# A two-layer decoder trunk: VectorE's steps of a pair in the up projection put in another order, one low part given to GpSimd, and the first two tiles of the down projection split earlier

## The chip, the core and the metric

One Trainium2 chip, one of its cores. The metric is the device time of one execution of the whole program in microseconds (us), the median of several runs. Engines: PE is TensorE (matmuls, with its weight loads), ACT is ScalarE, DVE is VectorE, POOL is GpSimd, and SP is SyncE, which issues the DMAs here. PE writes PSUM only; its eight banks are the tiles `pg` (four) and `pa` (four), each 128 x 512 in f32.

## The reference, cut to what matters

```python
def conv_ffn(h, w_up, conv_w, conv_b, w_down):
    u = causal_dwconv(h @ w_up, conv_w, conv_b)          # width 3
    a, g = jnp.split(u, 2, axis=-1)
    return (jax.nn.gelu(g, approximate=True) * a) @ w_down

for l in range(DEPTH):                                   # 2 layers
    h = hybrid_mixer(rmsnorm(x, pre_mix_g[l]), ...)
    x = x + rmsnorm(h, post_mix_g[l])
    h = memory_cross_attention(rmsnorm(x, pre_mem_g[l]), ...)
    x = x + rmsnorm(h, post_mem_g[l])
    h = conv_ffn(rmsnorm(x, pre_ffn_g[l]), w_up[l], fconv_w[l], fconv_b[l], w_down[l])
    x = x + rmsnorm(h, post_ffn_g[l])
```

512 tokens, width 1024, FFN width 2816, all in f32. The change concerns `conv_ffn` alone: `h @ w_up` (1024 to 5632 columns), the convolution over tokens with the gating, and the start of `@ w_down`.

## The kernel before, in words

**Precision.** A matmul operand is split in two fp32r parts: `hi` is a rounded copy made by ACT, `lo` is the source minus `hi`, made by DVE. `mm3` then issues three matmuls, hi.hi, hi.lo and lo.hi. A weight unit is a 128 x 1024 tile, loaded by SP into one of two `raw` buffers and split into one of five `whi` and five `wlo` buffers (`w_split`, `split`, L89 to L100).

**Up projection.** The 5632 columns are 22 pairs `j` of 128 linear columns (`a`, the unit `raws[j]`) and 128 gate columns (`g`, the unit `rgs[j]`, two buffers). Pairs 0 and 1 are done plainly (`feat_halves`). From pair 2 on, `up_products` takes a pair as a 2 x 2 block product (halves of the 1024 inputs by the two columns; tokens 0 to 255, "left", by 256 to 511, "right"), done with seven block products instead of eight. Its weight sides are `raws[j]` itself (kind `a`, products 1 and 2), the four sums of `add_up` (L1095 to L1098, on POOL: tiles `T`, kinds `t` for products 5 and 6 and `u` for 7 and 4), and half of `rgs[j]` (kind `b`, product 3, a single buffer `b`). `high(j, kind)` (L1105) casts the high part on ACT; `low(j, kind)` (L1116) subtracts on DVE. One product is 12 matmuls of 128 x 256. In iteration `j` of the loop (L1157) PE does product 5 of pair j, 4 of pair j-1, 6 of j, 1 of j+1, 2, 3 and 7 of j.

**What follows a pair.** Two PSUM tiles collect it, `A` (linear) and `G` (gate): `total(j)` alternates between two pairs of `pg` banks, so A and G of pair j are the banks of pair j-2. ACT's copy (L1161) and DVE's add (L1162) finish the right half of A and G of pair j-1; DVE's second add (L1183) prepares the left half of G of pair j, which product 3 then goes on with. `conv_first` (ACT, L1022) writes the first convolution term into `u`, `conv_rest` (DVE, L1027) adds two more from PSUM, ACT takes the gelu into G, and `gated` (DVE, L1041) multiplies into a tile of `gtiles`.

**Down projection.** `down` (L1202) takes the 22 `gtiles` in order. For tile k it splits the tile and a weight unit, then issues 24 matmuls of 128 x 512 into all eight banks: the four `pa` first, then the four `pg`, which are the banks of `total`: the first two those of pair 20, the last two those of pair 21.

**Order of work.** In `up_products` the order of ACT, DVE and POOL is the order of the code (`manual_schedule`, L1060), and so is SP's (L1062); every engine works its list in order and waits at the head. PE's order is that of the code throughout. Elsewhere a scheduler sets the order, so that pieces of the steps ahead of the loop mix with the end of `feat_halves`.

Of the kernel before, what the change touches and what calls it, by code (L numbers as in the profile page):

```python
# [23 lines left out]
NF = 22  # L24
# [14 lines left out]
def trunk_kernel(ctx: ExitStack, tc: tile.TileContext, x4, memt, w, gw, gains, mcw, fcw, gb,  # L39
# [111 lines left out]
    def run(gen):  # L151
        for _ in gen:
            tick()
# [856 lines left out]
    def ffn(l, xn, pend, forms):  # L1010
# [51 lines left out]
        with tc.manual_schedule(engines={mybir.EngineType.SP}):  # L1062
            run(up_products(l, fp, xn, forms, us, conv_first, conv_rest, gated))
        return es, order, gtiles

    def up_products(l, fp, xn, forms, us, conv_first, conv_rest, gated):
# [15 lines left out]
        def load_a(j):  # L1082
            if j < NF:
                raws[j] = load_raw(l, U_UP + 2 * j)

# [30 lines left out]
        def low(j, kind):  # L1116
            if j < NF:
                DVE.tensor_sub(ws[j, kind][1], source(j, kind), ws[j, kind][0].bitcast(F32))  # L1118
# [28 lines left out]
        for kind in "atu":  # L1147
            high(j0, kind)
            if kind != "u":
                low(j0, kind)  # L1150
# [3 lines left out]
        add_up(j0 + 1)  # L1154
        high(j0 + 1, "a")
        low(j0 + 1, "a")
        for j in range(j0, NF + 1):  # L1157
# [6 lines left out]
            load_g(j + 2)  # L1164
            load_a(j + 3)
# [7 lines left out]
            if p >= j0:  # L1173
                conv_rest(p, 1, G)
                yield from product(A[:, right], p, 4)
            low(j, "u")
            if p >= j0:
# [3 lines left out]
            if real:  # L1181
                yield from product(e1s[j], j, 6)
                DVE.tensor_add(total(j)[1][:, left], e1s[j], p5s[j])  # L1183
            high(j + 1, "t")
            low(j + 1, "t")
            if p >= j0:
                gated(p, us.pop((p, 0)), G)
            if j + 1 < NF:
# [5 lines left out]
            add_up(j + 2)  # L1194
            if real:
                yield from product(total(j)[0][:, left], j, 2)
                high(j + 1, "u")
                yield from product(total(j)[1][:, left], j, 3)
                high(j + 1, "b")
                yield from product(e1s[j], j, 7)  # L1200

    def down(l, forms, gtiles, consume, order):  # L1202
# [8 lines left out]
        for k in range(NF):  # L1211
            if k < 2:
                both = forms.flat(F32R)
                gh_, gl_ = both[:, :512], both[:, 512:]
# [4 lines left out]
            split(gtiles[k], gh_, gl_)  # L1219
            wu = load_unit(l, U_DOWN + k)  # L1220
# [18 lines left out]
    for l in range(L):  # L1239
# [30 lines left out]
        es, order, gtiles = ffn(l, xn, pend, forms)  # L1270
# [3 lines left out]
        run(down(l, forms, gtiles, tail.consume, order))  # L1274
# [83 lines left out]
```

## Time and profile before

| | us |
|---|---|
| median of 3 runs | 1593.67 |
| lowest, highest | 1593.04, 1596.27 |
| the profiled execution, its own time | 1599.54 |
| its span, first to last instruction | 1597.8 |

Busy in the span: PE 98% (a busy PE is not a PE at its peak, since matmuls are pipelined), DVE 71%, ACT 56%, POOL 22%. The up projections of the two layers run from about 480 to 685 us and from 1265 to 1464, the down projections from there to about 800 and 1577. Times in the rows further down are microseconds from the start of the span. Within a stretch the rows of one engine stand one behind the other; "[2.99 <-DVE u L1027]" is idle time of the engine just before the instruction and what ended it. In names, `wlo<-T,whi` is an instruction that writes a tile `wlo` and reads `T` and `whi`.

### The profile page before, as it was taken

To read this page: it belongs to the slowest core of one execution; us is meant where nothing else is said; L and a number is where in the kernel's file an instruction comes from. 1 tells how busy PE (TensorE), PEld (TensorE's weight loads), DVE (VectorE), ACT (ScalarE), POOL (GpSimd) and SP (SyncE) were. 2 spreads that over 40 slices of the span, in tenths; PEclk is the share of its full clock that TensorE was granted. 3 is DMA by queue.
4 is the path that set the end of the run, shared out by engine and by line. 5 is a ranking of instruction groups with operands and counts; after the bars stand their busy time and mean duration, and the time that the engine had idled before them with its cause. 6 is when DMAs were issued, how large, how long until landed. Compare 5 with 4: busy or idle time off the path is not lost.

```text
span 1597.8 us, 24498 instructions
## 1 busy us (share of the span) xinstructions
PE 1559.1 (98%) x9480; PEld 1377.3 (86%) x9480; DVE 1128.3 (71%) x1848; ACT 899.3 (56%) x1578; POOL 348.8 (22%) x252
## 2 busy tenths in 40 slices
PE   7999999999999999989999999999999999998998
PEld 5788888988899999978887888889888899997886
DVE  5687655746699999953376885557557999997433
ACT  5677574544466666642257775745445666665321
POOL 0000210100035676500010002101001567771000
PEclk9999999999999999999999999999999999999999
DMA  5422344552243332233323223444412223332321
GB/s 174 127 94 73 92 140 147 167 180 66 67 148 106 100 106 97 95 108 103 106 92 111 90 73 105 135 145 154 161 41 69 93 100 101 105 107 75 123 97 62
DMA packets 55431, 173.13 MB, mean 108 GB/s; under 512 B 6802, under 2 KB 9618, under 8 KB 55315
## 3 DMA queue, kind: packets, MB, share of 16 engines
q1 hardware_dynamic: 55314, 171.57, 33.0%
q8 instruction: 74, 1.21, 0.3%
q14 instruction: 43, 0.34, 0.1%
HBM read 165.22 MB, written 6.33 MB: 107 GB/s over the span
## 4 chain that ended last, share of the span: by engine, by line
PE 75%; DVE 11%; DMA 6%; ACT 4%; issue 2%; POOL 1%; SPq 0%; POOLq 0%; DVEq 0%; ACTq 0%
PE pg L107 47%; PE pa L107 26%; DMA raw<-in_w_dram 3%; DVE u L1027 2%; PE pa L111 2%; DVE wlo L1118 2%; DVE wlo L100 1%; ACT whi L99 1%; DMA raw<-in_memt_dram 1%; ACT junk L231 1%; DVE xg L252 1%; POOL sm L226 1%; DVE b L1118 1%; DMA raw<-dv 1%; DVE x L365 1%
## 5 line engine op out<-in xcount | busy, mean ns | idle before, releaser
L107 PE MATMUL pg<-B,whi 128*128 128x256 f32 (+1 forms) x1800 | 420.7, 327 | 8.9 <-DVE ql L991 4.0
L100 DVE TENSOR_TENSOR wlo<-raw,whi 128x1024 fp32r<-128x1024 f32 x188 | 231.3, 1231 | 223.6 <-ACT whi L99 223.2
L99 ACT CAST whi<-raw 128x1024 fp32r<-128x1024 f32 x188 | 197.6, 1052 | 226.0 <-PE pg L107 141.7
L107 PEld LDWEIGHTS pg<-B,whi 128*128 128x128 f32 x1800 | 291.0, 189 | 28.6 <-DVE ql L991 4.4
L107 PE MATMUL pg<-whi,B 128*128 128x512 f32 x896 | 297.8, 399 | 0.0
L107 PE MATMUL pg<-B,wlo 128*128 128x256 f32 (+1 forms) x896 | 288.7, 322 | 0.0
L107 PEld LDWEIGHTS pg<-whi,B 128*128 128x128 f32 x896 | 168.6, 188 | 35.1 <-DVE B L100 1.3
L226 POOL TENSOR_TENSOR sm<-sm,mhalf 128x1 f32<-128x1 f32 x56 | 34.4, 614 | 750.7 <-DVE sm L351 572.6
L107 PEld LDWEIGHTS pg<-B,wlo 128*128 128x128 f32 x896 | 168.8, 188 | 13.7
L107 PE MATMUL pg<-wlo,B 128*128 128x512 f32 x448 | 175.3, 391 | 0.6 <-DVE sm L244 0.6
L107 PE MATMUL pa<-S,whi 128*128 128x256 f32 x960 | 175.6, 283 | 0.0
L107 PEld LDWEIGHTS pa<-S,whi 128*128 128x128 f32 x960 | 148.4, 189 | 0.0
L1027 DVE SCALAR_TENSOR_TENSOR u<-pg,fcw,u 128x511 f32<-128x511 f32 (+1 forms) x176 | 130.7, 745 | 7.3 <-ACT u L1022 4.2
L107 PE MATMUL pa<-S,wlo 128*128 128x256 f32 x480 | 135.8, 283 | 0.0
L1118 DVE TENSOR_TENSOR wlo<-T,whi 128x1024 fp32r<-128x1024 f32 x80 | 125.6, 1569 | 0.0
L107 PE MATMUL pa<-whi,S 128*128 128x512 f32 x320 | 105.9, 390 | 0.0
L107 PE MATMUL pg<-whi,S 128*128 128x512 f32 x320 | 105.4, 390 | 0.0
L1022 ACT ACTIVATE u<-pg,fcw 128x512 f32<-128x512 f32 x88 | 68.6, 780 | 57.6 <-DVE pg L1162 32.0
L107 PEld LDWEIGHTS pg<-wlo,B 128*128 128x128 f32 x448 | 84.7, 189 | 15.7 <-DVE wlo L100 1.0
L107 PEld LDWEIGHTS pa<-S,wlo 128*128 128x128 f32 x480 | 90.9, 189 | 0.0
L1114 ACT CAST whi<-T 128x1024 fp32r<-128x1024 f32 x80 | 83.5, 1044 | 9.4 <-POOL T L1098 5.2
L1095 POOL TENSOR_TENSOR T<-rg,raw 128x512 f32<-128x512 f32 x40 | 55.4, 1385 | 136.7 <-DMA rg<-in_w_dram 101.6
(264 smaller groups left out, 3043.2 us busy)
## 6 DMA issues: line engine op xcount, KB each, us to landing
raw<-in_w_dram SPq DMA_DIRECT2D x228, 512.0 KB, 3.6
rg<-in_w_dram SPq DMA_DIRECT2D x40, 512.0 KB, 3.5
gain<-in_gains_dram SPq DMA_DIRECT2D x11, 512.0 KB, 5.3
raw<-in_memt_dram SPq DMA_DIRECT2D x20, 256.0 KB, 2.9
tb<-tb_d SPq DMA_DIRECT2D x16, 256.0 KB, 3.5
x<-in_x_dram SPq DMA_DIRECT2D x8, 256.0 KB, 5.7
e<-nmu_d SPq DMA_DIRECT2D x8, 256.0 KB, 3.9
dv<-vf SPq DMA_DIRECT2D x8, 256.0 KB, 4.4
```

Of the source, the lines that this page charges most:

```text
L99: ACT.copy(hi, src)
L100: DVE.tensor_sub(lo, src, hi.bitcast(F32))
L107: PE.matmul(o, lhs, rhs, **kw)
L111: PE.transpose(o, src, idn)
L226: POOL.tensor_tensor(r, v, mhalf[:, :1], ALU.pow)
L231: ACT.activation(junk[:, :src.shape[-1]], src, AF.Square, accum_out=s_)
L252: DVE.scalar_tensor_tensor(xg, xt[:, c], r, g[h], ALU.mult, ALU.mult)
L1022: ACT.activation(u, acc, AF.Identity, bias=fcw_t[:, m, 3:4], scale=fcw_t[:, m, 2:3])
L1027: DVE.scalar_tensor_tensor(u[:, q:], acc[:, :512 - q], fcw_t[:, m, 2 - q:3 - q], u[:, q:], ALU.mult, ALU.add)
L1095: POOL.tensor_tensor(t12[:, :512], b12, b11, ALU.subtract)
L1114: ACT.copy(ws[j, kind][0], source(j, kind))
L1118: DVE.tensor_sub(ws[j, kind][1], source(j, kind), ws[j, kind][0].bitcast(F32))
```

## The change

It edits `up_products` and `down` (with `ffn` and `run` only handing a list through):

- `low(j, "b")` is done by POOL instead of DVE. The other low parts stay on DVE.
- DVE's order within an iteration: the low part of `u` moves from between the two convolutions of an iteration to the end of the iteration before, behind those of `t` and `a`; the gating product of pair j-1 moves one iteration on, between the two convolutions.
- `add_up` of pair j+1 stands at the start of iteration j, behind POOL's low part of `b`; it stood in the middle of iteration j-1. SP's loads of iteration j still come after that low part and, for `raw`, after those sums.
- The weight units of down tiles 0 and 1 are loaded by the loop of the up projection, and `down_tile` splits both tiles and units in iteration 21, ahead of the last two iterations' convolution and gating.

```diff
...
@@ -1082,6 +1086,8 @@
         def load_a(j):
             if j < NF:
                 raws[j] = load_raw(l, U_UP + 2 * j)
+            elif j < NF + 2:
+                raws[j] = load_raw(l, U_DOWN + j - NF)
 
         def load_g(j):
             if j < NF:
@@ -1114,8 +1120,15 @@
             ACT.copy(ws[j, kind][0], source(j, kind))
 
         def low(j, kind):
-            if j < NF:
-                DVE.tensor_sub(ws[j, kind][1], source(j, kind), ws[j, kind][0].bitcast(F32))
+            if j >= NF:
+                return
+            sub = POOL.tensor_tensor if kind == "b" else DVE.tensor_tensor
+            sub(ws[j, kind][1], source(j, kind), ws[j, kind][0].bitcast(F32), ALU.subtract)
+
+        def down_tile(k):
+            both = forms.flat(F32R)
+            split(gtiles[k], both[:, :512], both[:, 512:])
+            return both[:, :512], both[:, 512:], w_split(raws.pop(NF + k))
 
         def total(j):
             i = 2 * (j % 2)
@@ -1146,14 +1159,13 @@
         load_a(j0 + 2)
         for kind in "atu":
             high(j0, kind)
-            if kind != "u":
-                low(j0, kind)
+            low(j0, kind)
         high(j0, "b")
         yield from first(j0)
         ACT.copy(total(j0)[0][:, left], e1s[j0])
-        add_up(j0 + 1)
         high(j0 + 1, "a")
         low(j0 + 1, "a")
+        ready = []
         for j in range(j0, NF + 1):
             p, real = j - 1, j < NF
             if p >= j0:
@@ -1162,6 +1174,7 @@
                 DVE.tensor_add(G[:, right], e1s[p], p5s[p])
             low(j, "b")
             load_g(j + 2)
+            add_up(j + 1)
             load_a(j + 3)
             if p >= j0:
                 conv_first(p, 1, G)
@@ -1172,34 +1185,37 @@
                 ACT.copy(p5s[j], e5)
             if p >= j0:
                 conv_rest(p, 1, G)
+                if p > j0:
+                    gated(p - 1, us.pop((p - 1, 0)), total(p - 1)[1])
                 yield from product(A[:, right], p, 4)
-            low(j, "u")
-            if p >= j0:
                 conv_first(p, 0, A)
                 ACT.activation(G, us.pop((p, 1)), AF.Gelu_apprx_tanh)
                 conv_rest(p, 0, A)
-            if real:
-                yield from product(e1s[j], j, 6)
-                DVE.tensor_add(total(j)[1][:, left], e1s[j], p5s[j])
+            if not real:
+                gated(p, us.pop((p, 0)), G)
+                return ready
+            yield from product(e1s[j], j, 6)
+            DVE.tensor_add(total(j)[1][:, left], e1s[j], p5s[j])
             high(j + 1, "t")
             low(j + 1, "t")
-            if p >= j0:
-                gated(p, us.pop((p, 0)), G)
-            if j + 1 < NF:
+            if j + 1 == NF:
+                ready.append(down_tile(0))
+            else:
                 yield from first(j + 1)
             high(j + 2, "a")
             low(j + 2, "a")
             if j + 1 < NF:
                 ACT.copy(total(j + 1)[0][:, left], e1s[j + 1])
-            add_up(j + 2)
-            if real:
-                yield from product(total(j)[0][:, left], j, 2)
-                high(j + 1, "u")
-                yield from product(total(j)[1][:, left], j, 3)
-                high(j + 1, "b")
-                yield from product(e1s[j], j, 7)
-
-    def down(l, forms, gtiles, consume, order):
+            yield from product(total(j)[0][:, left], j, 2)
+            high(j + 1, "u")
+            low(j + 1, "u")
+            if j + 1 == NF:
+                ready.append(down_tile(1))
+            yield from product(total(j)[1][:, left], j, 3)
+            high(j + 1, "b")
+            yield from product(e1s[j], j, 7)
+
+    def down(l, forms, gtiles, consume, order, ready):
         accs = [[pg() for _ in range(4)], [pa() for _ in range(4)]]
         held = []
 
@@ -1210,14 +1226,13 @@
 
         for k in range(NF):
             if k < 2:
-                both = forms.flat(F32R)
-                gh_, gl_ = both[:, :512], both[:, 512:]
+                gh_, gl_, wu = ready[k]
             else:
                 if k % 2 == 0:
                     both = forms.wide(F32R).rearrange("p (a b) t -> p a (b t)", a=4)
                 gh_, gl_ = both[:, k % 2, :], both[:, 2 + k % 2, :]
-            split(gtiles[k], gh_, gl_)
-            wu = load_unit(l, U_DOWN + k)
+                split(gtiles[k], gh_, gl_)
+                wu = load_unit(l, U_DOWN + k)
             if k < NF - HELD:
                 for h in (1, 0):
                     for t in range(4):
...
```

How the order of the instructions moves, at three places (line numbers of the changed kernel are 4 to 15 higher).

**DVE, one iteration of layer 0 in the middle of the loop**, from the add that finishes G to the last step before the next such add. `pg` are A and G, `u` the convolved columns, `wlo<-T` the low parts of `t` and `u`, `wlo<-raw` that of `a`, `b` that of `b`, and `B<-u,pg` the gating product. Before:

```order
L1162 TENSOR_TENSOR pg_4939<-pa_5289,p_1103_5376 128x256
L1118 TENSOR_TENSOR b_5468<-rg_5230,b_5468 128x512
L1027 SCALAR_TENSOR_TENSOR u_5489<-pg_4939,fcw_4652,u_5489 128x511
L1027 SCALAR_TENSOR_TENSOR u_5489<-pg_4939,fcw_4652,u_5489 128x510
L1118 TENSOR_TENSOR wlo_5454<-T_5308,whi_5453 128x1024
L1027 SCALAR_TENSOR_TENSOR u_5521<-pg_4938,fcw_4652,u_5521 128x511
L1027 SCALAR_TENSOR_TENSOR u_5521<-pg_4938,fcw_4652,u_5521 128x510
L1183 TENSOR_TENSOR pg_4937<-pa_5417,p_1120_5504 128x256
L1118 TENSOR_TENSOR wlo_5540<-T_5435,whi_5539 128x1024
L1041 TENSOR_TENSOR B_5415<-u_5521,pg_4939 128x512
L1118 TENSOR_TENSOR wlo_5558<-raw_5359,whi_5557 128x1024
```

And now:

```order
L1174 TENSOR_TENSOR pg_4939<-pa_5288,p_1103_5376 128x256
L1031 SCALAR_TENSOR_TENSOR u_5488<-pg_4939,fcw_4652,u_5488 128x511
L1031 SCALAR_TENSOR_TENSOR u_5488<-pg_4939,fcw_4652,u_5488 128x510
L1045 TENSOR_TENSOR B_5507<-u_5393,pg_4937 128x512
L1031 SCALAR_TENSOR_TENSOR u_5521<-pg_4938,fcw_4652,u_5521 128x511
L1031 SCALAR_TENSOR_TENSOR u_5521<-pg_4938,fcw_4652,u_5521 128x510
L1198 TENSOR_TENSOR pg_4937<-pa_5415,p_1119_5503 128x256
L1126 TENSOR_TENSOR wlo_5540<-T_5480,whi_5539 128x1024
L1126 TENSOR_TENSOR wlo_5557<-raw_5359,whi_5556 128x1024
L1126 TENSOR_TENSOR wlo_5574<-T_5481,whi_5573 128x1024
```

The low part of `b` is gone (POOL's list has it ahead of the four sums); the five steps with PSUM between the two adds stand together, and the three low parts stand behind the second add.

**DVE, layer 0, end of the loop**, from the second add of pair 21. `T<-B` and `wlo<-raw` at L100 are the low parts of the first two down tiles and their weight units. Before:

```order
L1183 TENSOR_TENSOR pg_4939<-pa_7321,p_1356_7394 128x256
L1041 TENSOR_TENSOR gt_7429<-u_7411,pg_4937 128x512
L1162 TENSOR_TENSOR pg_4939<-pa_7321,p_1356_7394 128x256
L1027 SCALAR_TENSOR_TENSOR u_7469<-pg_4939,fcw_4652,u_7469 128x511
L1027 SCALAR_TENSOR_TENSOR u_7469<-pg_4939,fcw_4652,u_7469 128x510
L1027 SCALAR_TENSOR_TENSOR u_7485<-pg_4938,fcw_4652,u_7485 128x511
L1027 SCALAR_TENSOR_TENSOR u_7485<-pg_4938,fcw_4652,u_7485 128x510
L1041 TENSOR_TENSOR gt_7490<-u_7485,pg_4939 128x512
L100 TENSOR_TENSOR T_7509<-B_4872,T_7509 128x512
L100 TENSOR_TENSOR wlo_7515<-raw_7512,whi_7514 128x1024
L100 TENSOR_TENSOR T_7542<-B_4872,T_7542 128x512
L100 TENSOR_TENSOR wlo_7548<-raw_7545,whi_7547 128x1024
```

And now:

```order
L1198 TENSOR_TENSOR pg_4939<-pa_7323,p_1357_7397 128x256
L100 TENSOR_TENSOR T_7433<-B_4872,T_7433 128x512
L100 TENSOR_TENSOR wlo_7437<-raw_7141,whi_7436 128x1024
L100 TENSOR_TENSOR T_7452<-B_4872,T_7452 128x512
L100 TENSOR_TENSOR wlo_7456<-raw_7266,whi_7455 128x1024
L1174 TENSOR_TENSOR pg_4939<-pa_7323,p_1357_7397 128x256
L1031 SCALAR_TENSOR_TENSOR u_7485<-pg_4939,fcw_4652,u_7485 128x511
L1031 SCALAR_TENSOR_TENSOR u_7485<-pg_4939,fcw_4652,u_7485 128x510
L1045 TENSOR_TENSOR gt_7489<-u_7415,pg_4937 128x512
L1031 SCALAR_TENSOR_TENSOR u_7503<-pg_4938,fcw_4652,u_7503 128x511
L1031 SCALAR_TENSOR_TENSOR u_7503<-pg_4938,fcw_4652,u_7503 128x510
L1045 TENSOR_TENSOR gt_7508<-u_7503,pg_4939 128x512
```

The four splitting steps stood behind the last gating product and now stand ahead of the add that finishes pair 21; the gating of pair 20 moved behind that add.

**DVE, layer 1, where pair 2 begins**: the last convolution terms of pairs 0 and 1 (`u<-pg`), with the low parts of pair 2 between them. Before:

```order
L1027 SCALAR_TENSOR_TENSOR u_12723<-pg_12518,fcw_12491,u_12723 128x511
L1118 TENSOR_TENSOR wlo_12817<-T_12804,whi_12816 128x1024
L1027 SCALAR_TENSOR_TENSOR u_12723<-pg_12518,fcw_12491,u_12723 128x510
L1027 SCALAR_TENSOR_TENSOR u_12754<-pg_12519,fcw_12491,u_12754 128x511
L1027 SCALAR_TENSOR_TENSOR u_12754<-pg_12519,fcw_12491,u_12754 128x510
L1041 TENSOR_TENSOR B_12728<-u_12695,u_12723 128x512
L1027 SCALAR_TENSOR_TENSOR u_12782<-pg_12520,fcw_12491,u_12782 128x511
L1027 SCALAR_TENSOR_TENSOR u_12782<-pg_12520,fcw_12491,u_12782 128x510
```

And now:

```order
L1031 SCALAR_TENSOR_TENSOR u_12723<-pg_12518,fcw_12491,u_12723 128x511
L1126 TENSOR_TENSOR wlo_12817<-T_12804,whi_12816 128x1024
L1031 SCALAR_TENSOR_TENSOR u_12723<-pg_12518,fcw_12491,u_12723 128x510
L1031 SCALAR_TENSOR_TENSOR u_12754<-pg_12519,fcw_12491,u_12754 128x511
L1126 TENSOR_TENSOR wlo_12821<-T_12805,whi_12820 128x1024
L1031 SCALAR_TENSOR_TENSOR u_12754<-pg_12519,fcw_12491,u_12754 128x510
L1045 TENSOR_TENSOR B_12728<-u_12695,u_12723 128x512
L1031 SCALAR_TENSOR_TENSOR u_12782<-pg_12520,fcw_12491,u_12782 128x511
L1031 SCALAR_TENSOR_TENSOR u_12782<-pg_12520,fcw_12491,u_12782 128x510
```

A second low part, that of `u`, stands between the last terms, three rows behind that of `t`.

## Rows read from the trace of the kernel before

**Rows 1.** Waits, PE, whole program: line waited for: us in total, times, longest.
```profile
PE pa L107 <- ACT whi L99: 6.7, 2, 3.3
PE pg L107 <- DVE pg L1183: 3.8, 8, 0.6
PE pg L107 <- DVE u L1027: 3.4, 3, 3.0
PE pa L107 <- DVE wlo L100: 2.1, 2, 1.1
```

**Rows 2.** Busy time by stage: us, PE (x) PEld DVE ACT POOL, granted clock, DMA.
```profile
692.00:694.00 2.00, 2.00 (x6) 1.55 (x5) 1.14 (x2) 0.00 (x0) 0.00 (x0) 0.50 0.81 279
...
1260.00:1270.00 10.00, 10.00 (x74) 9.92 (x74) 8.97 (x10) 7.01 (x11) 1.84 (x2) 0.87 0.32 102
...
1280.00:1455.00 175.00, 174.59 (x1455) 173.78 (x1454) 170.64 (x192) 114.69 (x173) 122.72 (x66) 1.00 0.31 103
```

**Rows 3.** Timeline, PE, end of up and start of down: start, us, instruction.
```profile
685.44 0.28 PE L107 MATMUL pg<-B,wlo 128*128 128x256 f32 x1
...
695.71 0.55 PE L107 MATMUL pg<-whi,T 128*128 128x512 f32 x1
...
1464.37 0.28 PE L107 MATMUL pg<-B,wlo 128*128 128x256 f32 x1
...
1474.48 0.39 PE L107 MATMUL pg<-whi,T 128*128 128x512 f32 x1
```

**Rows 4.** Chain of waits: start, us, PE matmuls in a row.
```profile
632.83 2.85 PE pa L107 x24
...
701.50 2.72 PE pg L107 x12
```

**Rows 5.** Timeline, ACT, copy L1161: first and last interval of each layer.
```profile
489.13 0.36 ACT L1161 COPY pg<-pa 128x256 f32<-128x256 f32 x1 [0.81 <-PE pa L107]
...
674.30 0.36 ACT L1161 COPY pg<-pa 128x256 f32<-128x256 f32 x1 [0.80 <-PE pa L107]
...
1270.84 0.36 ACT L1161 COPY pg<-pa 128x256 f32<-128x256 f32 x1 [0.81 <-PE pa L107]
...
1453.22 0.36 ACT L1161 COPY pg<-pa 128x256 f32<-128x256 f32 x1 [0.81 <-PE pa L107]
```

**Rows 6.** Groups by line: busy us, mean ns of one | idle before.
```profile
L1027 DVE SCALAR_TENSOR_TENSOR u<-pg,fcw,u 128x511 f32<-128x511 f32 (+1 forms) x176 | 130.7, 745 | 7.3 <-ACT u L1022 4.2
...
L1041 DVE TENSOR_TENSOR B<-u,pg 128x512 f32<-128x512 f32 x28 | 18.9, 676 | 0.0
...
L1183 DVE TENSOR_TENSOR pg<-pa,p 128x256 f32<-128x256 f32 x40 | 17.0, 424 | 0.0
...
L1022 ACT ACTIVATE u<-pg,fcw 128x512 f32<-128x512 f32 x88 | 68.6, 780 | 57.6 <-DVE pg L1162 32.0 <-PE pg L107 25.6
```

**Rows 7.** Timeline, DVE and POOL, layer 0: start, us, instruction.
```profile
477.14 1.31 POOL L1097 TENSOR_TENSOR T<-rg 128x512 f32<-128x512 f32 x1
...
507.32 2.08 DVE L1118 TENSOR_TENSOR wlo<-T,whi 128x1024 fp32r<-128x1024 f32 x1
508.40 2.17 POOL L1096 TENSOR_TENSOR T<-rg,T 128x512 f32<-128x512 f32 x1
...
661.03 1.22 DVE L1118 TENSOR_TENSOR wlo<-T,whi 128x1024 fp32r<-128x1024 f32 x1
...
665.05 0.68 DVE L1118 TENSOR_TENSOR b<-rg,b 128x512 fp32r<-128x512 f32 x1
```

**Rows 8.** Timeline, where the pairs begin in layers 0 and 1.
```profile
476.33 2.98 DVE L1027 SCALAR_TENSOR_TENSOR u<-pg,fcw,u 128x511 f32<-128x511 f32 x4 [1.50 <-ACT u L1022]
...
478.01 0.48 PE L107 MATMUL pg<-B,whi 128*128 128x512 f32 x1 [0.28 <-DVE u L1027]
...
1255.36 2.22 DVE L1118 TENSOR_TENSOR wlo<-T,whi 128x1024 fp32r<-128x1024 f32 x1
...
1258.38 0.47 PE L107 MATMUL pg<-B,whi 128*128 128x512 f32 x1 [2.99 <-DVE u L1027]
```

More of the change, by code (lines that the diff above doesn't have):

```diff
@@ L151, in run @@
     def run(gen):
-        for _ in gen:
+        while True:
+            try:
+                next(gen)
+            except StopIteration as end:
+                return end.value
             tick()
@@ L1062, in ffn, with up_products @@
         with tc.manual_schedule(engines={mybir.EngineType.SP}):
-            run(up_products(l, fp, xn, forms, us, conv_first, conv_rest, gated))
-        return es, order, gtiles
-    def up_products(l, fp, xn, forms, us, conv_first, conv_rest, gated):
+            ready = run(up_products(l, fp, xn, forms, us, conv_first, conv_rest, gated, gtiles))
+        return es, order, gtiles, ready
+    def up_products(l, fp, xn, forms, us, conv_first, conv_rest, gated, gtiles):
         j0 = 2
@@ L1269, in trunk_kernel @@
         forms = tail.forms
-        es, order, gtiles = ffn(l, xn, pend, forms)
+        es, order, gtiles, ready = ffn(l, xn, pend, forms)
         last = l == L - 1
@@ L1273, in trunk_kernel @@
         tail.open()
-        run(down(l, forms, gtiles, tail.consume, order))
+        run(down(l, forms, gtiles, tail.consume, order, ready))
         xn = tail.xn
```

## Prediction, made before the changed kernel ran

> **What bounds the kernel now.** I read the waits of TensorE (PE) first, then the table by stage, then single stretches of the timeline. In the table, the long middle of layer 1's up projection has PE busy in 174.59 of 175 us and VectorE (DVE) in 170.64, with GpSimd (POOL) at 122.72 [rows 2]. So PE is the bound there, DVE stands close behind it, and a change can only win what PE still loses. PE's waits list three places in the FFN [rows 1]: on ScalarE's (ACT's) `whi` and DVE's `wlo` casts, twice each (once per layer, where the down projection begins), on DVE's add L1183 eight times (inside the pairs), and on the convolution L1027 three times (where the pairs begin). After the first of these the granted clock reads 0.50, the lower level of 1.2 GHz, where the rest of the stage has the full 2.4 GHz; in 10 us after the wait at 1258 it reads 0.87 [rows 2]. Before each fall PE had stood idle, so an idle stretch is paid for twice.
>
> **The change, part by part.** PE's own order is the same in both kernels; only what the other engines do for it moves. The sum is made against the profiled execution, 1599.54 us (span 1597.8). That is 5.9 us above the median of 1593.67; I carry the difference in time over to the median; if some of the stalls below are the profiled execution's own, the gain is smaller, which the range's upper part takes in.
>
> *1. The start of the down projection.* A 128x256 matmul follows its predecessor after 2.85/24 = 0.119 us, a 128x512 one after 2.72/12 = 0.227 [rows 4]. In layer 0 the last up matmul starts at 685.44; twelve down matmuls into the `pa` banks should follow and the first into a `pg` bank start at 685.44+0.12+2.72 = 688.28. It starts at 695.71: 7.43 us lost. In layer 1: 1464.37+0.12+2.72 = 1467.21 against 1474.48, 7.27 lost [rows 3]. Together 14.7, part idle, part half clock.
> With the change both first tiles are split while PE does the last pair's products 2, 3 and 7. I count from the start of product 5 of that pair, a product taking 12 x 0.119 = 1.43. Six products end at 8.55; the copy L1161 and product 4 bring PE to about 10.6 (estimate). DVE has its add done at 6.0, four splitting subtractions, 2 x (0.68+1.22) = 3.8 [rows 7], end at 9.8. Then the add (0.42), ACT's first convolution term (0.78), two DVE terms (1.49), the gating product (0.68), two more terms and a second gating product [rows 6]: 10.2, 11.0, 12.5, 13.2, 14.7, 15.4. PE writes `pa` until 13.3, then four `pg` banks at 13.3, 14.0, 14.7 and 15.4; the last three are freed at 13.2, 14.7 and 15.4. It just fits: I leave 0.35 us per layer and book **-14.0**. Bounds: -14.7, and -12.7 if DVE comes 1 us late in each layer. The transfers come earlier too: SP issues both tiles' loads with the pairs' own and the second tile's split no longer waits behind the last gating.
>
> *2. Inside the pairs.* The copy L1161 stands once per pair. Eighteen intervals take 674.30-489.13 = 185.17 us in layer 0 and 1453.22-1270.84 = 182.38 in layer 1 [rows 5]; 84 matmuls of 0.11875 make 9.975, eighteen pairs 179.55. PE loses 5.62 and 2.83, 8.45 in all, 0.23 a pair.
> Why it loses this: product 3 starts 5 x 1.425 = 7.1 us into a pair and needs the add L1183. On DVE there stand before it an add, a low part of `b`, two convolution terms, the low part of `u`, two terms. A low part takes 1.22 alone and 2.08 when a POOL operation holds it up, and POOL's take 2.17 against 1.31 [rows 7]. Next to the convolution, which reads PSUM, POOL keeps its 1.31 [rows 7, 8]: four terms from 476.33 on take 2.98 with POOL's 1.31 at 477.14. So only the low parts collide.
> With the change the stretch is add 0.42, wait for ACT 0.78, terms 1.49, gating 0.68, terms 1.49, add 0.42 [rows 6]: 5.3, from about 0.7 to 6.0, 1.1 us ahead of product 3. The three low parts follow, 3 x 1.22, to 9.7. POOL's five operations, 5 x 1.31 = 6.5, start when the `b` cast allows, some 0.4 before the pair's first product, and end near 6.1: beside DVE's PSUM work. The sums are due when ACT casts `t` (about 4.5) and `u` (about 6.9); they are there at 3.5 and 6.1. The loads keep more than 3 us of slack: the gate's weights are asked for once POOL's low part is done and used a whole pair later. I book **-7.7** of the 8.45; bounds -8.45 and -4.
> The `b` low part costs DVE 0.68 alone [rows 7] and POOL about 1.31, as the sums show. That is 0.6 more for each of 40. The Trainium skill (GPSIMD Engine Reference, Engine selection) advises against just this: two-input elementwise work runs about twice as long on GpSimd as on VectorE. Put on the path it would be +25 us, and the sum +3; I book 0 for it, because POOL stands idle 52 of 175 us [rows 2] and product 3 needs the part only at 7.1, six microseconds after it should be done.
>
> *3. The last product 3 of each layer* comes one product sooner, at 5.7, against an add at 6.0: the longest wait of 0.6 [rows 1] shrinks to some 0.4. **-0.3**, bounds -1.0 and 0.
>
> *4. Where the pairs begin.* DVE now does the low part of `u` ahead of the last FFN convolution terms, and POOL's sums for pair 3 move behind its low part. Layer 0: DVE waited 1.50 for ACT at 476.33 [rows 8]; the low part fits in but for 0.5, so the bank PE waits for at 478.01 comes 0.5 later, and later ones up to 1.2: +0.8. Layer 1: the low part of `t` at 1255.36 took 2.22, 1.00 more than alone, because POOL was in its sums; without these PE's 2.99 us wait ends about 1 us sooner [rows 8], and perhaps the clock holds. The inserted low part then delays the fourth bank: -0.5. Together **+0.3**; bounds -1.9 (a clock that holds gives 1.5 more) and +2.2.
>
> Sum: -14.0 -7.7 -0.3 +0.3 = **-21.7**, 1593.67-21.7 = **1572.0 us**. All good bounds give -26.0, all bad ones -14.5: 1567.6 to 1579.2.
>
> **The rivals.**
> *A. The port stays full.* POOL's five operations and DVE's three low parts exclude each other for their whole length: 5 x 1.31 + 3 x 1.22 = 10.2 us, more than 9.975, and no better than today's (185.17+182.38)/36 = 10.21. Term 2 is then about -0.4, the sum -14.4: **1579.3**. For it: every collision in rows 7 costs nearly a whole operation. Against it: 10.2 counts start and end of each operation as locked, and a collision at 508 cost both engines 0.86, not 1.2 or 1.3. The Trainium skill (SBUF — State Buffer, Who interferes with whom) says that a VectorE instruction with two SBUF inputs and a GpSimd one that reads SBUF exclude each other for the whole instruction; by that rule rival A is the outcome, and the trace agrees on who collides.
> *B. Down starts, but waits one bank on.* If a tile's load or ACT is late, DVE reaches the last two gatings 2 us late or more, PE stands before the third `pg` bank, the clock falls again: half of term 1 is gone, **1579.0**. The row for it is DVE's thin fit above; against it stands that ACT's casts of both tiles are ordered ahead of all that PE waits for there.
> *C. Slower.* POOL's work spills into DVE's low parts. No POOL operation of this trace writes fp32r, so the price of the moved part is unknown. DVE's own round is 5.3+3.66 = 8.96 us; each collision adds 2.08-1.22 = 0.86. One gives 9.82, still under 9.975; from the second on DVE is the bound: two 10.68, three 11.54. Three, with term 1 kept, give 36 x (11.54-10.21) - 14 = +34, about **1628**; two give +3, **1597**. It decides when POOL ends later than about 8 us into the pair, that is when the moved part takes more than 3 us. Against it: DVE writes 512 columns of fp32r in 0.68 and of f32 in 0.676 [rows 6, 7], and POOL's work starts anew with each `b` cast, beside PSUM work.
>
> **How the numbers follow.** Forecast 0.72, A 0.11, B 0.08, C 0.06, and 0.03 that gains and losses cancel. About 0.2% (3.2 us) is what a measurement of this kernel can tell from no change. Forecast, A and B are all faster by more: 0.91. C slower, 0.06; same 0.03. The range reaches from just below the forecast's good end to past A and B: 1567 to 1581; the forecast's tails, C and the cancelling case lie outside.
>
> **What would show it.** In the changed profile: PE's waits on `whi` and `wlo` at the start of down gone and the clock 1.00 there; L1161's counterpart every 9.97 to 10.0 us; PE's waits on the second add gone except at each layer's last pair; DVE's low parts near 1.22 and POOL's operations near 1.31; POOL's low part of `b` at about 1.3. Wrong would be: low parts still at 1.6 to 2.1 in the mean (A), a wait of PE on a gating or convolution after the first twelve down matmuls (B), the moved part at 3 us or more, or pairs above 10.2 (C).

## The result, and the profile after

| | before | changed |
|---|---|---|
| median of 6 runs, us | 1594.97 (1593.04 to 1600.01) | 1575.37 (1571.36 to 1576.06) |
| profiled execution, us (span) | 1599.54 (1597.8) | 1576.06 (1574.3) |

The ratio is 0.9868, 95% interval 0.9849 to 0.9887: 19.6 us less by the medians, 21.7 forecast. The two profiled executions differ by 23.5; the one of before lay 4.6 us above its median, the changed one 0.7.

PE's waits in the changed kernel, the FFN's lines (line waited for: us in total, times, longest):

```profile
PE pg L107 <- DVE u L1031: 2.8, 2, 2.0
PE pa L107 <- DVE wlo L1126: 2.2, 2, 1.2
PE pg L107 <- ACT pg L1173: 0.9, 2, 0.4
```

The waits on `whi` and `wlo` at the start of down and those on the second add [rows 1] are gone. The wait on the convolution is still there, and one on a low part, L1126, is new: once in each layer, where the pairs begin.

Busy time by stage of the changed kernel (columns as in [rows 2]):

```profile
682.00:684.00 2.00, 2.00 (x10) 1.67 (x9) 1.97 (x4) 1.79 (x3) 0.00 (x0) 1.00 0.13 51
1240.00:1250.00 10.00, 7.87 (x50) 7.37 (x49) 9.62 (x11) 6.44 (x9) 8.25 (x6) 0.83 0.32 105
1260.00:1435.00 175.00, 175.00 (x1477) 175.00 (x1476) 138.40 (x177) 114.55 (x176) 112.18 (x88) 1.00 0.32 107
```

In 175 us of layer 1's pairs PE is never idle, and DVE is busy for 138.40 where it was for 170.64 [rows 2]. Of those 32 us the moved step would account for 17.5 x 0.68 = 12, had it run undisturbed [rows 7]; the other 20 were collisions with POOL, which have gone. The granted clock is 1.00 at the start of down, where it was 0.50. At the start of layer 1's pairs it still falls, to 0.83 in the mean.

Timeline of the changed kernel, PE at the start of down (both layers), ACT's copy (the first and the last interval of each layer, as in [rows 5]):

```profile
680.74 0.29 PE L107 MATMUL pg<-B,wlo 128*128 128x256 f32 x1
...
683.61 0.39 PE L107 MATMUL pg<-whi,T 128*128 128x512 f32 x1
...
1448.19 0.28 PE L107 MATMUL pg<-B,wlo 128*128 128x256 f32 x1
...
1451.05 0.39 PE L107 MATMUL pg<-whi,T 128*128 128x512 f32 x1
...
490.71 0.36 ACT L1173 COPY pg<-pa 128x256 f32<-128x256 f32 x1 [0.81 <-PE pa L107]
...
670.14 0.36 ACT L1173 COPY pg<-pa 128x256 f32<-128x256 f32 x1 [0.80 <-PE pa L107]
...
1258.17 0.36 ACT L1173 COPY pg<-pa 128x256 f32<-128x256 f32 x1 [0.80 <-PE pa L107]
...
1437.59 0.36 ACT L1173 COPY pg<-pa 128x256 f32<-128x256 f32 x1 [0.81 <-PE pa L107]
```

Eighteen intervals take 179.43 and 179.42 us, 9.97 a pair. From the last up matmul to the first one into a `pg` bank it is 2.87 and 2.86 us; 2.84 is what the matmuls between them take (0.12 + 12 x 0.227, [rows 4]).

Groups by line of the changed kernel (busy us, mean ns | idle before):

```profile
L1126 DVE TENSOR_TENSOR wlo<-T,whi 128x1024 fp32r<-128x1024 f32 x80 | 103.9, 1299 | 9.7 <-ACT whi L1120 9.7
L1103 POOL TENSOR_TENSOR T<-rg 128x512 f32<-128x512 f32 x40 | 54.7, 1367 | 6.4 <-DVE S L100 6.4
L1126 POOL TENSOR_TENSOR b<-rg,b 128x512 fp32r<-128x512 f32 x40 | 51.6, 1290 | 142.7 <-ACT b L1120 142.7
```

The same two groups of the kernel before:

```profile
L1118 DVE TENSOR_TENSOR wlo<-T,whi 128x1024 fp32r<-128x1024 f32 x80 | 125.6, 1569 | 0.0
...
L1097 POOL TENSOR_TENSOR T<-rg 128x512 f32<-128x512 f32 x40 | 81.0, 2025 | 11.1 <-DVE S L100 6.4 <-DVE wlo L1118 4.6
```

Low parts of `t` and `u` take 1.30 in the mean where they took 1.57, and POOL's third sum 1.37 where it took 2.03: close to the 1.22 and 1.31 of such steps undisturbed [rows 7]. The moved step takes 1.29 on POOL.

Where the two spans part, by the copies that begin the pairs: up to the first of layer 0 +1.58; its 18 intervals -5.74; the interval behind them -0.54 (9.32 became 8.78); from there to the first of layer 1 -7.97; its 18 intervals -2.96; the next -0.55; from the last copy to the end -7.32. The sum is -23.50.

### The profile page after: what moved, and what is told of

Read it like the earlier page. It is cut to its first block, busy times and chain, and to the rows that moved or that the text cites. A ratio compares the mean times of both kernels' runs of the same rounds, so it can differ in the third digit from the quotient of the medians.

```text
span 1574.3 us, 24497 instructions
## 1 busy us (share of the span) xinstructions
PE 1547.4 (98%) x9480; PEld 1371.0 (87%) x9480; DVE 1049.2 (67%) x1808; ACT 892.0 (57%) x1578; POOL 326.5 (21%) x292
## 3 DMA queue, kind: packets, MB, share of 16 engines
q8 instruction: 74, 1.21, 0.3%
## 4 chain that ended last, share of the span: by engine, by line
PE 82%; DVE 6%; DMA 5%; ACT 3%; issue 2%; POOL 1%; SPq 0%; POOLq 0%; DVEq 0%; ACTq 0%
PE pg L107 51%; PE pa L107 28%; PE pa L111 2%; DMA raw<-in_w_dram 2%; DVE wlo L100 1%; DMA raw<-in_memt_dram 1%; ACT whi L99 1%; DVE xg L256 1%; POOL sm L230 1%; ACT junk L235 1%; DVE x L369 1%; DMA raw<-dk 1%; DVE wlo L1126 1%; DMA raw<-dv 1%; DMA dk<-kf 0%
## 5 line engine op out<-in xcount | busy, mean ns | idle before, releaser
L100 DVE TENSOR_TENSOR wlo<-raw,whi 128x1024 fp32r<-128x1024 f32 x188 | 230.6, 1228 | 215.7 <-ACT whi L99 213.1
L107 PEld LDWEIGHTS pg<-B,wlo 128*128 128x128 f32 x896 | 168.9, 188 | 13.6
L1126 DVE TENSOR_TENSOR wlo<-T,whi 128x1024 fp32r<-128x1024 f32 x80 | 103.9, 1299 | 9.7 <-ACT whi L1120 9.7
L1126 POOL TENSOR_TENSOR b<-rg,b 128x512 fp32r<-128x512 f32 x40 | 51.6, 1290 | 142.7 <-ACT b L1120 142.7
```

The lines of the kernel that those rows point to most:

```text
L100: DVE.tensor_sub(lo, src, hi.bitcast(F32))
L107: PE.matmul(o, lhs, rhs, **kw)
```

## The experiments

Each kernel ran beside the kernel before, whose median was 1596.6 to 1597.6 us in these runs. I compare ratios to it; 0.001 is 1.6 us. "A pair" is the mean of the 36 intervals in the trace: 10.21 us in the kernel before, 9.97 in the changed one.

### The two halves apart

**e1_down_late**: the changed kernel without the early down tiles.

```diff
...
             high(j + 1, "t")
             low(j + 1, "t")
-            if j + 1 == NF:
-                ready.append(down_tile(0))
-            else:
+            if j + 1 < NF:
...
-            if j + 1 == NF:
-                ready.append(down_tile(1))
...
```

> The changed kernel, with the first two down tiles loaded and split where they were before, behind the last gating product; the rest of the change stays. Theory (the start of the down projection is the larger half of the gain): 14 to 15 us slower than the changed kernel, so about 1590; in the profile PE waits at the start of each down projection on ACT's and DVE's casts for 3.3 and 1.1 us, the granted clock there falls to 0.5, and the pairs stay at 9.97 us. Rival (the pairs carry the gain, the start of down is covered by them): at most 5 us slower than the changed kernel, about 1580.

Measured: 1593.5 us, ratio 0.9973 (0.9961 to 0.9985), so 0.0105 or 16.7 us above the changed kernel, where 14 to 15 was expected. Its timeline, PE at the start of down:

```profile
685.89 0.49 PE L107 MATMUL pa<-whi,T 128*128 128x512 f32 x1 [3.34 <-ACT whi L99]
...
688.28 0.80 PE L107 MATMUL pa<-wlo,T 128*128 128x512 f32 x1 [1.90 <-DVE wlo L100]
```

And the busy time by stage there:

```profile
690.00:692.00 2.00, 2.00 (x6) 1.52 (x6) 0.56 (x1) 0.23 (x1) 0.00 (x0) 0.50 0.80 242
```

Waits and half clock are back, and a pair stays at 9.97: the pairs don't depend on the early tiles. The second wait is 1.90 us where it was 1.1 at most [rows 1], so without the early tiles the new order makes the start of down a little worse than it was.

**e2_down_early_only**: the kernel before with `down_tile`, the early loads for it and the two calls of it that e1 took out.

> The kernel before, with only the early splitting of the first two down tiles added. Theory: 14 us faster than before, about 1580.5, no half clock at the start of down, and the pairs stay at 10.1 to 10.3 us in the mean. Rival (without the new order DVE is too late with the last pair, so PE waits one bank further on): 7 us faster or less, with a wait of PE on a gating product or a convolution after the first twelve down matmuls.

Measured: 1584.25 us, ratio 0.9915 (0.9898 to 0.9932): 13.6 us faster. A pair is 10.24 there, as before. The early tiles alone give 13.6 us and the pairs alone, e1's 0.0027, give 4.3: 17.9 against the 21 of 0.9868, with 2 to 3 us of uncertainty in each; e1's longer wait at the start of down takes from the 4.3.

### What the pairs owe to which part

**e3_b_on_dve**: the changed kernel with `b`'s low part on DVE.

```diff
-            sub = POOL.tensor_tensor if kind == "b" else DVE.tensor_tensor
+            sub = DVE.tensor_tensor
```

> The changed kernel, with the low part of b done by DVE again; the new order, POOL's later sums and the early down tiles stay. Order theory (what counts is that DVE's SBUF steps and POOL's steps do not meet, and DVE has room): the part fits DVE's 0.8 us wait for ACT at the start of the pair, though POOL's sums now meet it and it takes 1.2 to 1.5; pairs at 9.97 to 10.0, within 2 us of the changed kernel. Work theory (what counts is that DVE has less to do): pairs at 10.1 to 10.2, 5 to 8 us slower than the changed kernel.

Measured: 1625.12 us, ratio 1.0168 (1.0138 to 1.0198). Both theories missed: 0.68 us a pair moved back costs 1.46 a pair, which is now 11.43. One pair of it in the timeline of SP's queue, POOL, DVE and ACT:

```profile
563.25 0.33 SPq L1095 DMA_DIRECT2D rg<-in_w_dram  x1
...
567.37 1.94 POOL L1101 TENSOR_TENSOR T<-rg,raw 128x512 f32<-128x512 f32 x1 [3.03 <-DMA rg<-in_w_dram]
569.38 2.16 POOL L1102 TENSOR_TENSOR T<-rg,T 128x512 f32<-128x512 f32 x1
...
568.05 2.33 DVE L1126 TENSOR_TENSOR wlo<-raw,whi 128x1024 fp32r<-128x1024 f32 x1
570.31 2.32 DVE L1126 TENSOR_TENSOR wlo<-T,whi 128x1024 fp32r<-128x1024 f32 x1
...
570.54 0.36 ACT L1173 COPY pg<-pa 128x256 f32<-128x256 f32 x1 [0.80 <-PE pa L107]
```

The stage in e3:

```profile
520.00:640.00 120.00, 108.09 (x867) 106.25 (x866) 119.26 (x115) 68.50 (x105) 84.48 (x42) 0.97 0.29 94
```

And the same place in the changed kernel:

```profile
569.73 1.29 POOL L1126 TENSOR_TENSOR b<-rg,b 128x512 fp32r<-128x512 f32 x1 [3.53 <-ACT b L1120]
570.98 1.30 POOL L1101 TENSOR_TENSOR T<-rg,raw 128x512 f32<-128x512 f32 x1
...
574.88 1.31 POOL L1104 TENSOR_TENSOR T<-raw,T 128x512 f32<-128x512 f32 x1
...
570.46 0.36 ACT L1173 COPY pg<-pa 128x256 f32<-128x256 f32 x1 [0.80 <-PE pa L107]
...
575.61 0.42 DVE L1198 TENSOR_TENSOR pg<-pa,p 128x256 f32<-128x256 f32 x1
575.95 1.32 DVE L1126 TENSOR_TENSOR wlo<-T,whi 128x1024 fp32r<-128x1024 f32 x1
...
578.60 1.23 DVE L1126 TENSOR_TENSOR wlo<-T,whi 128x1024 fp32r<-128x1024 f32 x1 [0.20 <-ACT whi L1120]
```

In the changed kernel the sums start 0.52 us behind the copy that begins the pair (570.98 against 570.46), because POOL's own low part stands ahead of them and waits for ACT's cast of `b`. They end when DVE's low parts begin. In e3 nothing in POOL's list waits for that cast. The sums start as soon as their load has come, 4.1 us after its issue, and that is 3.17 us ahead of the copy: in the midst of DVE's low parts. Two of these take 2.3 us each, DVE is busy 119.26 of 120 us, and PE waits 34.5 us in all for the second add. Without collisions DVE's steps, `b`'s among them, would come to 0.42 + 0.68 + 1.49 + 0.68 + 1.49 + 0.42 + 3 x 1.22 = 8.8 us of work a pair, less than PE's 9.97. So by these rows the moved step does not earn its place by the 0.68 us that it takes off DVE; it holds the sums back. No run holds the sums back in another way with `b` on DVE, so this is read from the rows and not tested by itself.

**e12_grouping_only**: e3 with `add_up(j + 2)` also back in the iteration before.

> Grouping alone: the changed kernel with the low part of b back on DVE and POOL's sums back in the iteration before; early down tiles stay. If the grouping is good by itself, PE is still fed: at most the 1584 of the kernel with early down tiles and the old order. If what counts is where POOL's sums fall, they start some 5.5 us into the pair, when the load that waits for b has come, run through all three low parts, and three collisions make DVE's round 9.6 + 3 x 0.86 to 1.1 less its waits: about 11 us a pair, 1610 to 1630.

Measured: 1625.88 us, ratio 1.0184 (1.0164 to 1.0203), a pair 11.42, as the second theory had it, and the same as e3. Where the sums stand in POOL's list does nothing as long as no step of POOL waits for `b`: here they start 4.67 us ahead of the copy (567.07 against 571.74).

**e4_sums_early**: the changed kernel with the sums in the iteration before, ahead of POOL's low part.

```diff
...
             load_g(j + 2)
-            add_up(j + 1)
             load_a(j + 3)
...
                 ACT.copy(total(j + 1)[0][:, left], e1s[j + 1])
+            add_up(j + 2)
```

> The changed kernel, with POOL's four sums put back to the middle of the iteration before, so that they run beside DVE's three low parts; DVE's order and the low part of b on POOL stay. Order theory, by the price of the forecast's rival C (0.86 us for each collision on a DVE round of 8.96): three collisions per pair, low parts at about 2.1 us, pairs at 10.7 (two count) to 11.5 us (three), 26 to 55 us slower than the changed kernel. Work theory: DVE has only 8.2 us of work per pair, pairs at 9.97 to 10.1, at most 5 us slower.

Measured: 1609.9 us, ratio 1.0087 (1.0054 to 1.0119), a pair 11.03. The order theory holds in size, but not by its reason: of DVE's three low parts in the pair below only the first collides (1.88 us, then 1.21 twice), where it had three collisions. PE's waits name the place:

```profile
PE pg L107 <- POOL b L1126: 28.0, 21, 3.8
```

The timeline of POOL and DVE shows the loop:

```profile
566.56 1.31 POOL L1101 TENSOR_TENSOR T<-rg,raw 128x512 f32<-128x512 f32 x1 [3.85 <-DMA rg<-in_w_dram]
...
571.72 1.30 POOL L1126 TENSOR_TENSOR b<-rg,b 128x512 fp32r<-128x512 f32 x1
...
576.92 1.31 POOL L1101 TENSOR_TENSOR T<-rg,raw 128x512 f32<-128x512 f32 x1 [3.89 <-DMA rg<-in_w_dram]
...
572.23 1.88 DVE L1126 TENSOR_TENSOR wlo<-T,whi 128x1024 fp32r<-128x1024 f32 x1
```

The sums wait for a load, the low part for the sums, and the next load for the low part. One round from 566.56 to 576.92 is 10.36 us here, and longer where a low part of DVE falls on it. The mean hides three kinds of pairs: some of 9.97 (that of these rows is one), most of 10.9 to 11.6, and three of 14.6 to 15.2; what makes the longest is open.

**e5_b_on_pool_only**: the kernel before with `b`'s low part on POOL, and nothing else.

> The kernel before with one edit: POOL does the low part of b; order and down projection as before. Work theory (DVE's 0.68 us per pair is what counts): DVE's round falls from 10.2 to some 9.5 us, under PE's 9.975, and the pairs' 8 us are won: about 1589.5 against 1597.5 for the kernel before. Order theory (what counts is when POOL works): POOL comes to b only after four sums, some 2.5 us later than DVE did, beside DVE's low part of u (1.22 becomes 2.08); the gate's load that waits for b, and the next sums with it, come later by as much. Then nothing is won and the pairs grow to 10.3 to 11 us: 1600 to 1625.

Measured: 1655.24 us, ratio 1.0358 (1.0327 to 1.0388). The order theory had the sign, and was too small by 30 us. It is e4's loop with collisions in it: one round, sums to sums, is 12.85 us long (POOL L1101 at 572.06 and at 584.91, of which 4.38 wait for the load), and a pair takes 11.87 in the mean. PE waits 42.7 us for POOL's `b`.

**e9_old_dve_order**: the changed kernel with DVE's order of before.

```diff
                 conv_rest(p, 1, G)
-                if p > j0:
-                    gated(p - 1, us.pop((p - 1, 0)), total(p - 1)[1])
                 yield from product(A[:, right], p, 4)
+            low(j, "u")
...
             low(j + 1, "t")
+            if p >= j0:
+                gated(p, us.pop((p, 0)), G)
...
             high(j + 1, "u")
-            low(j + 1, "u")
```

> The changed kernel with DVE's order of before: the low part of u between the two convolutions, the gating product behind the low part of t. POOL's low part of b, its sums just in time and the early down tiles stay. If the grouping matters, the low part of u meets POOL's sums in every pair (2.1 to 2.3 us for 1.22), the second add ends at about 7.1 us into the pair where product 3 wants it at 6.9: 0.2 to 0.5 us a pair, 1583 to 1593. If one collision in a pair fits into DVE's slack: 1575 to 1578.

Measured: 1578.31 us, ratio 0.9889 (0.9872 to 0.9905), at the edge of what the second theory allowed and 3.3 us above the changed kernel, with intervals that overlap. In the trace a pair is 10.07 and the last interval of a layer 9.32, as before: 3.7 + 1.1 = 4.8 us. The low part of `u` does meet the third sum in every pair (2.03 us at 573.18), and DVE has room for it. So by the traces the larger part of the pairs' gain, 10.24 in e2 to 10.07 here, comes from POOL's step and the sums behind it, and 10.07 to 9.97, with the last product 3, from the grouping (DVE's PSUM steps together, its low parts behind them). That is one trace of each: the ratios of e2 and e9 overlap too.

### How much room is left on POOL

**e7_low_a_on_pool**: `kind in "ab"` in place of `kind == "b"`.

> The changed kernel with the low part of a (128x1024) on POOL too. POOL then has 5 x 1.31 + about 2.6 = 9.1 us of a pair, DVE keeps two low parts, 2 x 1.22. If SBUF operations of the two exclude each other for their whole length, a pair needs 9.1 + 2.4 = 11.5 us: 36 x 1.55 more, about 1630. If only what really falls together costs 0.86 us a time, DVE's round is at most 5.3 + 2 x 2.08 = 9.5 us, under PE's 9.975, and the time stays within some 10 us of the changed kernel: 1575 to 1585.

Measured: 1608.39 us, ratio 1.0068 (1.0049 to 1.0086), a pair 10.70. Both missed, from either side. POOL is busy 119.14 of 120 us in the pairs and is the bound; the 128x1024 step takes 3.18 in the mean. At 576.55 it takes 3.38, beside DVE's low part of `t`, which starts at 575.30; what it takes alone no run shows.

**e10_one_more_sum**, **e11_two_more_sums**: POOL's third sum done twice, and three times.

```diff
-                POOL.tensor_tensor(t34[:, :512], b22, b12, ALU.subtract)
+                for _ in range(2):
+                    POOL.tensor_tensor(t34[:, :512], b22, b12, ALU.subtract)
```

> The changed kernel with one needless POOL operation in each pair: the third of the four sums is done twice (1.3 us, same values). POOL then ends at about 7 us into the pair and meets one low part of DVE. By the prediction's rival C one collision of 0.86 to 1.1 us fits (9.8 to 10.0 us a round against PE's 9.975): 1575 to 1578. By its rival A, exclusion over whole operations counted as a sum, a pair needs 6 x 1.31 + 3 x 1.22 = 11.5 us: about 1630.

> The same with the third sum done three times, two needless operations in each pair. POOL ends at about 8.5 us into the pair, past the 8 us from which rival C decides, and meets two low parts; the cast of u that waits for the last sum comes 1.3 us late. By C DVE's round is 10.7 to 11.0 us and DVE is the bound: 36 x 0.7 to 1.0, 1600 to 1612. By the sum of whole operations 7 x 1.31 + 3 x 1.22 = 12.8 us: about 1677. If both still fit beside PE: 1575.

Measured: 1645.73 us, ratio 1.0310 (1.0294 to 1.0325), and 1698.74, ratio 1.0642 (1.0626 to 1.0657); pairs of 11.78 and 13.14 us. One operation of 1.3 us more costs 1.8 us a pair, and "one collision fits" is wrong. Rival A's sums of whole operations, 1630 and 1677, come nearer, and are still 16 and 22 us short. One round of e10 on POOL, ACT, DVE and PE:

```profile
573.88 1.81 POOL L1127 TENSOR_TENSOR b<-rg,b 128x512 fp32r<-128x512 f32 x1 [1.68 <-ACT b L1121]
...
578.30 3.64 POOL L1104 TENSOR_TENSOR T<-rg 128x512 f32<-128x512 f32 x2
581.91 2.27 POOL L1105 TENSOR_TENSOR T<-raw,T 128x512 f32<-128x512 f32 x1
...
584.21 1.04 ACT L1121 CAST whi<-T 128x1024 fp32r<-128x1024 f32 x1 [3.57 <-POOL T L1105]
585.16 0.61 ACT L1121 CAST b<-rg 128x512 fp32r<-128x512 f32 x1
...
580.69 2.33 DVE L1127 TENSOR_TENSOR wlo<-raw,whi 128x1024 fp32r<-128x1024 f32 x1
...
586.10 0.51 PE L107 MATMUL pg<-B,whi 128*128 128x256 f32 x2 [1.74 <-ACT pg L1174]
```

It is a closed ring: POOL's low part and sums, ACT's cast of `u`, which needs the last sum, then ACT's cast of `b` behind it in its queue, then POOL's next low part. From 573.88 to 585.85 it takes 11.97 us. POOL's part, from its low part to the end of the fourth sum, is 10.3 us and not the changed kernel's 6.46: 1.27 for the operation, and 0.5 + 1.1 + 0.96 for collisions of the low part, the third and the fourth sum that it brings. PE stands for 1.74 us on the copy, which is behind these casts in ACT's list. DVE is not the bound, it is busy for 88 of 120 us. In the changed kernel the last sum ends at 576.19 and ACT casts `u` at 577.52, when PE lets it: 1.3 us of room in the ring, used up by one operation.

### The start of the pairs

**e6_low_u_later**: the first pair's low part of `u` goes behind that of the next pair's `a`.

```diff
             high(j0, kind)
-            low(j0, kind)
+            if kind != "u":
+                low(j0, kind)
...
         low(j0 + 1, "a")
+        low(j0, "u")
```

> The changed kernel with the first pair's low part of u behind the low part of the next pair's a, four rows of DVE's list in each layer. If the two new waits of PE on a low part at the start of the pairs (0.99 us in layer 0, 1.25 in layer 1) come from that order, they go: 1575.4 - 2.2 = about 1573. If they come from POOL's sums standing beside these low parts, the collision moves to another row and PE waits as long: 1575.

Measured: 1574.76 us (1572.14 to 1578.23), ratio 0.9862 (0.9840 to 0.9883): not told apart from the changed kernel's 0.9868. In the trace layer 1's wait on the low part is gone and layer 0's is 1.25 us for 0.99, so each theory holds in one layer; the span is 1572.4, 1.9 less.

**e8_banks_behind_first_product**: e6, and in `first` the matmuls that open banks A and G behind `product(e1s[j], j, 1, True)`.

> The kernel of the run before with the low part of u later, and in the first two pairs the matmuls that open the PSUM banks A and G stand behind product 1 and not ahead of it, so PE does 1.43 us of other work before it needs the convolution's banks. If the wait on the convolution (0.84 us in layer 0, 1.98 in layer 1) and the half clock behind it are lost time, they shrink or go: 2.2 + 0.8 + 1.4 + up to 1.5 less than the changed kernel's 1575.4, that is 1569.5 to 1571. If DVE's convolution sets when the first pair can end, the wait only moves to the next product: 1573 to 1575.

Measured: 1576.88 us (1573.61 to 1578.96), ratio 0.9867 (0.9849 to 0.9886). Nothing is won. The pairs of layer 0 take 10.08 in this trace, with PE busy throughout; why is open. PE's waits at the start, which e6 had brought from 5.0 to 3.6 us, are 5.6:

```profile
PE pa L107 <- DVE wlo L1126: 3.5, 2, 2.1
...
PE pa L107 <- ACT pg L1166: 1.2, 1, 1.2
...
PE pg L107 <- DVE u L1031: 0.9, 1, 0.9
```

The wait on the convolution goes from 2.8 to 0.9 and comes back on the low part of `a`, so it seems that PE waits for DVE's whole list there and not for one bank. No version beat the changed kernel by more than the runs can tell.

## Why the prediction came out, point by point

The time, 1575.37, is 3.4 us above the point and inside the range; 1.3 of the 3.4 is the median of the kernel before, which six runs put at 1594.97 and not 1593.67. By the two traces:

| term | forecast | traces |
|---|---|---|
| 1 start of down | -14.0 | -14.65 |
| 2 pairs | -7.7 | -8.70 |
| 3 last product 3 | -0.3 | -1.09 |
| 4 where pairs begin | +0.3 | +2.39 |

The sum of the last column is -22.05 of the 23.5 us between the profiled executions. The rest lies outside of the four places, 1.3 us of it between the two layers' FFNs, most of it in steps that the change leaves alone. There the kernel before has this wait, which no other trace kept here has:

```profile
PE pa L111 <- DVE sig L800: 0.6, 1, 0.6
```

The medians show 3.9 less than the profiled executions; no run here says in which term. That the four terms add up to so nearly the forecast is in part luck: 1 to 3 won 2.4 us more than I booked, and 4 lost 2.1 more, which is outside its bounds.

**Term 1** was right as reasoned. What [rows 3] lost, 7.43 and 7.27 us, is 0.03 and 0.02 now (680.74 + 2.84 = 683.58 against 683.61). The 0.35 us per layer that I had left for a thin fit on DVE wasn't needed. e2 gains 13.6 us by it alone, and e1 loses 16.7 by taking it out.

**Term 2** came out whole: 179.43 us is below even the 179.55 that I had taken as the floor. Second adds end at 576.03 and product 3 starts at 577.38, 1.35 ahead where I had 1.1. The reasons were half right. That POOL beside DVE's PSUM steps costs neither of them anything is what the traces show: in the pair above the sums beside them take 1.30 to 1.32 us, and DVE's convolution terms take 0.747 in the mean, for 0.745 before [rows 6]. But I booked POOL's low part as a load moved to an idle engine at no cost, with 52 idle us of 175 as its cover. e3 and e12 show that it is the step that holds the sums in their place; e4, 35 us above the changed kernel, and e5, 59 above the kernel before, what it costs where it stands behind the sums; and e10 that POOL's idle time was no cover: 1.3 us more of work don't fit. The Trainium skill's advice to keep two-input elementwise work off GpSimd (GPSIMD Engine Reference, Engine selection) has the right ratio here, 1.29 against 0.68 us. Its verdict depends on the order: e3, which follows it, is 3% slower than the changed kernel, and e5, which goes against it in the old order, 3.6% slower than the kernel before.

**Term 3** had the right sign. I had DVE reach the last add of a layer 0.4 late; it is in time, both last intervals fell by 0.54 and 0.55. e9, without the grouping, has 9.32 there again, so the grouping gives this.

**Term 4** was mis-sized in layer 0 and came out as a loss in layer 1. In layer 0, PE stops for the convolution at 477.67 (478.51 - 0.84) where it stopped at 477.73 [rows 8], and the first copy stands at 490.71 for 489.13 [rows 5]: +1.64 for +0.8. The bank that PE waits for came 0.56 later (0.84 for 0.28 us), near my 0.5. What I had as "later ones up to 1.2" was not a bank but the low part of pair 3's `a`, a wait of its own:

```profile
478.51 0.48 PE L107 MATMUL pg<-B,whi 128*128 128x512 f32 x1 [0.84 <-DVE u L1031]
...
480.78 1.77 POOL L1103 TENSOR_TENSOR T<-rg 128x512 f32<-128x512 f32 x1
...
482.73 2.16 DVE L1126 TENSOR_TENSOR wlo<-raw,whi 128x1024 fp32r<-128x1024 f32 x1
...
484.94 0.39 PE L107 MATMUL pa<-B,wlo 128*128 128x256 f32 x1 [0.99 <-DVE wlo L1126]
...
1243.95 0.47 PE L107 MATMUL pg<-B,whi 128*128 128x512 f32 x1 [1.98 <-DVE u L1031]
...
1252.40 0.39 PE L107 MATMUL pa<-B,wlo 128*128 128x256 f32 x1 [1.25 <-DVE wlo L1126]
```

These rows are the changed kernel's timeline where the pairs begin. POOL's sums for that pair, now later, fall on DVE's low part, which takes 2.16 us for 1.22. In layer 1 the wait of 2.99 [rows 8] is 1.98, the 1 us that I had named, but 1.25 us are given back on the low part, and the clock did not hold (0.83). PE stops there at 1241.97 where it stopped at 1255.39, 13.42 earlier, and the first copy at 1258.17 is only 12.67 earlier: a loss of 0.75 where I had booked a gain of 0.5. One pair of traces does not settle a term of this size. In e2, whose steps there are those of the kernel before and whose wait is as long (3.00 us), the stretch from that stop to the first copy takes 16.69 us where it took 15.45, at a granted clock of 0.80 and not 0.89.

**The rivals.** A did not come: pairs are 9.97 and not 10.2. Its sum counts the edges of neighbours twice: in the pair shown the last sum ends at 576.19 and the low part starts at 575.95. But its idea, that the two engines' SBUF steps exclude each other, holds: DVE's low parts and POOL's five steps fill the pair from 569.73 to 579.83, one behind the other, which fits that e10 found no room. In e7 its sum overstates as well, 11.5 for 10.70, though 2.6 of it is an estimate that no run shows. My reason against A, that a collision cost 0.86 us and not a whole operation, was too favourable: in e3 it is 2.33 - 1.22 = 1.1. That is what the Trainium skill's exclusive lock (SBUF — State Buffer, Who interferes with whom) says, and the traces come near it: 1.1 is most of the 1.31 that a POOL step takes. B did not come. C did not come, since POOL's work ended 5.7 us behind the copy (576.19 against 570.46), where C wanted 8. Its threshold was wrong: I let the first collision be free and made DVE the bound from the second; in e10 one more operation brought three longer ones, and a ring through ACT set the time.

## What to carry to other kernels

Before a step is moved to an idle engine, ask what in that engine's queue it will hold back or let go: here the value of POOL's low part is that it pins four other steps beside work they don't collide with, and the same move without the new order lost 59 us. Where steps of two engines exclude each other, as DVE's low parts and POOL's steps do here, lay them out in one line over one round of the loop; idle time on either engine is room only where the other has no such step. And follow the ring from the moved step through the casts and loads that wait for it back to itself: its length, and no engine's busy share, was the next bound in e10.

## What the runs showed of the hardware that was not expected

POOL writes fp32r as fast as f32: 1.29 us for the low part of 128x512 against 1.31 for the last sum, both undisturbed. And a DVE subtraction of 128x1024 that meets a run of POOL's 128x512 steps took 2.33 us in e3 and e10 and 2.34 in e11, with one, two or three of them still to come: the time of about one POOL step more, whatever the run's length, in these rows. They read as if the two engines took turns, step by step: in e3 each step of either one behind the first takes about one step of the other longer (2.33 and 2.32 on DVE, 2.16 on POOL).
